# Gates o and z of the eighth head as seven products of blocks: the dense part, the attention's sums, and new orders

## The chip, the cores and the metric

The kernel runs on one core of a Trainium2 chip. A core has engines that each run their own list of instructions in order: TensorE (PE) multiplies matrices into PSUM, VectorE (DVE) and ScalarE (ACT) work on elements, GpSimd (POOL) does small things and issues those transfers that add into their target, and SyncE (SP) issues most other transfers (DMA). They wait for each other by semaphores. The metric is the device time of one execution in microseconds (us). The kernel before takes 1486.5 us, the median of three runs (1485.95 to 1486.61).

## The reference

Two layers work on 512 latent tokens of width 1024, with 256 context tokens beside them. Layer 0 mixes a long convolution (hyena) and a grouped attention; layer 1, which the change touches, is an mLSTM with 8 heads, run over the tokens in both directions. Cut to the second layer:

```python
q, k, v, o, z, gates = split(h @ w_in)          # o, z: 8 heads x 256 columns each
C = a_prev * C + (vc * a).T @ kc                # state of a head, chunk by chunk
num = s @ vc + w_prev * (C @ qc)
den = sum(s) + w_prev * (nvec @ qc)
h = num / max(abs(den), exp(-m))
h = (h_forward + h_backward) * sigmoid(o)
h = rms_norm(h, head_norm)
y = (h * silu(z)) @ w_out
x = x + gate * rms_norm(y, g_post)
```

So each head needs two gates from the layer's input: o (512 tokens x 256 columns) and z (the same), products with K = 1024. They are used only at the head's end.

## The kernel before, in words

Every fp32 product is made of three products of split numbers: a value is cast to a rounded part (names with h: `wh`, `hTh`, `vh`; a cast on ACT) and the rest (names with l: `wl`, `hTl`, `vl`; a subtraction on DVE), and `mm3` (L1013) multiplies h x h, h x l and l x h into PSUM. So each weight tile that arrives (`wr` or `ch`, 128 x 1024, 512 KB) costs one cast on ACT and one subtraction on DVE.

The program has regions: start, hyena, attention, the first output projection, the dense part of layer 1 (`l1a`), the heads (`l1b`) and the second output projection (`out1`). Each operation of a region is recorded, and `play()` (L993) issues them in an order that a table of numbers, `ORDERS`, writes out per region. All instructions therefore carry one line of the source, L998, and are told apart by their tiles. A second table says which buffer each tile gets.

In the dense part, `gates_oz(h)` (L2482) makes o and z of heads 0 to 6 together as a 2 x 2 problem of blocks. The tokens are halved, K is halved, and instead of eight block products it makes seven: the token operands are sums of blocks (`F3`, `F5`, `F6`, `D1`, made once), the weight operands are blocks or sums of blocks. The sums of weights (`o_sums` in DRAM, four per head) are made early in the program by `oz_sums` (L1633), eight steps, each one transfer per head: a copy on SP's queue or an accumulating transfer on POOL's. One of the seven products (`product`, L2469) is 2 token blocks x 4 k-blocks x 3 = 24 matmuls of 256 columns. The results are combined by sums on DVE, go through tanh or silu on ACT, and are put away in DRAM (`oz_scratch`).

`heads(h, H, N, before)` (L2544) runs head h. Per direction it forms the decay matrix `E`, the scaled keys `ka`, five state products v, ka (`pj`), the state `C` on DVE, its split `Ch` (ACT) and `Cl` (DVE), and for each of four token blocks a product v, E and a product C, q (`pm`), joined in `num`. Then `normed` rescales by the denominator into `hh`, multiplies with the gate `so`, takes squares (`hj`), the root (`hst`, `hrs`), and multiplies with `zs`; `result` transposes hh and puts it away in `y_scratch`. Between these, `fill()` takes pieces of work from a list: the next head's projections, or, in head 7, which has no next head and whose gates are not made in the dense part, its own gates. Those are plain products: `load_w` of two weights, four token blocks for each gate, 24 matmuls of 256 columns for each. Head 7 also makes the rows of the output modulation (`row`: 16 small matmuls each from 1 MB tiles of `w_mod`; `spread` sends a row to all tokens).

`out1` multiplies the heads' results with `o_w_out`, again with seven block products. Its operands come from `y_scratch` (`yraa`, `yrab`, `yfh`, `yfl`, the new content of `hTh`, `hTl`) and need many DVE subtractions of 128 x 512; the heads' region ends with its first two products (`p1`, `q7`).

Of the kernel before, what the change touches and what calls it, by code (L numbers as in the profile page):

```python
# [7 lines left out]
F32 = mybir.dt.float32  # L8
# [6 lines left out]
P = 128  # L15
# [136 lines left out]
class Ctx:  # L152
# [570 lines left out]

SLOTS = {
    "xt@0": [
        3, 5, 4, 0, 2, 1, 5, 3, 4, 0, 1, 5,
    ],
# [2166 lines left out]
```

## Time and profile before

| what | us |
|---|---|
| median of 3 runs | 1486.5 (1485.95 to 1486.61) |
| profiled execution | 1486.4 |
| its span | 1484.6 |
| 865 to 910: start of the dense part | PE busy 40.87 of 45, DVE 40.30 |
| 1320 to 1344: end of head 6 | PE 22.46 of 24, DVE 17.67, DMA share 0.89 |
| 1476 to 1484.6: after the last matmul | PE 0.31, DVE 5.17 |

The page names groups by engine, output tile and input tiles; `pj`, `pm`, `qst` and the like are names of the program. A row of a group ends with the idle time of the engine just before these instructions and with what ended most of it. A row of a timeline begins with the start and the duration of an instruction, and ends, in brackets, with the idle time before it. Matmuls overlap: their records are longer than the distance between their starts, so the starts tell the rate.

### The profile page before, as it was taken

The numbers are of one execution on the slowest core, as the hardware profiler recorded it, in microseconds if no ns is written. First come the engines' busy times: TensorE is split into PE (matmuls) and PEld (weight loads), VectorE is DVE, ScalarE is ACT, GpSimd is POOL, SyncE is SP. The second block draws the span as 40 slices with busy tenths as digits, with TensorE's granted clock in tenths as the row PEclk, the third lists the DMA queues.
The fourth block names the chain that finished last, engine by engine and source line by source line (L and its number), as shares of the span: only waits on it lengthen the run. The fifth ranks groups of instructions, "written<-read, shape, count | busy, mean of one in ns | idle before, by whom it ended". The sixth has DMA issues, their size and how long they took to land. (4 is left out here: it accounts for less than half of the span.)

```text
span 1484.6 us, 25597 instructions
## 1 busy us (share of the span) xinstructions
PE 1448.9 (98%) x10122; PEld 1320.5 (89%) x10122; DVE 1071.1 (72%) x1971; ACT 778.8 (52%) x1587; POOL 95.2 (6%) x141
## 2 busy tenths in 40 slices
PE   7999999999999999999999989999999999999997
PEld 5888998989998998989997779999999999989776
DVE  6687777887865666668334899666777777778698
ACT  5643443344435444446332567655766666766554
POOL 1100000001000000000000100000000101110000
PEclk9999999999999999999999999999999999999999
DMA  9655556557331121233463343676654647476575
GB/s 380 212 139 151 142 138 165 147 127 185 86 103 43 55 96 47 90 118 104 152 217 98 114 144 129 228 257 211 221 166 114 161 126 166 141 199 179 203 256 215
DMA packets 63687, 230.93 MB, mean 156 GB/s; under 512 B 7707, under 2 KB 9243, under 8 KB 60784
## 3 DMA queue, kind: packets, MB, share of 16 engines
q1 hardware_dynamic: 55000, 198.63, 38.9%
q0 software_dynamic: 7696, 29.50, 11.3%
q8 instruction: 79, 1.29, 0.3%
q10 hardware_dynamic: 872, 1.18, 0.2%
q14 instruction: 40, 0.33, 0.1%
HBM read 207.23 MB, written 68.19 MB: 186 GB/s over the span
## 5 line engine op out<-in xcount | busy, mean ns | idle before, releaser
L998 PE MATMUL pj<-wl,hTh 128*128 128x256 f32 (+2 forms) x1104 | 315.4, 291 | 1.9 <-DVE wl L998 1.9
L998 PE MATMUL pj<-wh,hTh 128*128 128x256 f32 (+2 forms) x1104 | 316.2, 293 | 0.8 <-ACT qjunk L998 0.4
L998 PE MATMUL pj<-wh,hTl 128*128 128x256 f32 (+2 forms) x1104 | 313.8, 291 | 0.0
L998 PE MATMUL pj<-hTh,wh 128*128 128x512 f32 (+1 forms) x832 | 286.7, 347 | 0.1
L998 PE MATMUL pj<-hTl,wh 128*128 128x512 f32 (+1 forms) x832 | 285.5, 344 | 0.6 <-DVE hTl L998 0.6
L998 PE MATMUL pj<-hTh,wl 128*128 128x512 f32 (+1 forms) x832 | 285.2, 345 | 0.0
L998 DVE TENSOR_TENSOR wl<-wr,wh 128x1024 fp32r<-128x1024 f32 (+1 forms) x154 | 187.6, 1222 | 48.5 <-ACT wh L998 45.7
L998 PEld LDWEIGHTS pj<-wl,hTh 128*128 128x128 f32 x1104 | 206.9, 189 | 7.4 <-DVE wl L998 2.9
L998 PEld LDWEIGHTS pj<-wh,hTh 128*128 128x128 f32 x1104 | 205.9, 188 | 7.4 <-issue 2.0
L998 PEld LDWEIGHTS pj<-wh,hTl 128*128 128x128 f32 x1104 | 206.0, 188 | 4.3 <-issue 1.1
L998 ACT CAST wh<-wr 128x1024 fp32r<-128x1024 f32 (+1 forms) x154 | 159.0, 1044 | 95.5 <-PE pj L998 61.7
L998 PEld LDWEIGHTS pj<-hTh,wh 128*128 128x128 f32 x832 | 156.6, 189 | 19.2 <-DVE vl L998 0.9
L998 PEld LDWEIGHTS pj<-hTh,wl 128*128 128x128 f32 x832 | 156.3, 188 | 18.2 <-DVE wl L998 0.2
L998 PEld LDWEIGHTS pj<-hTl,wh 128*128 128x128 f32 x832 | 156.7, 189 | 17.4 <-DVE hTl L998 0.9
L998 DVE TENSOR_TENSOR PTl<-pj,PTh 128x384 fp32r<-128x384 f32 (+1 forms) x80 | 41.1, 525 | 18.8 <-ACT PTh L998 18.3
L998 ACT CAST PTh<-pj 128x384 fp32r<-128x384 f32 (+1 forms) x80 | 35.5, 458 | 30.6 <-PE pj L998 30.0
L998 DVE TENSOR_TENSOR wl<-ch,wh 128x1024 fp32r<-128x1024 f32 x28 | 34.2, 1221 | 24.1 <-ACT wh L998 24.0
L998 DVE TENSOR_REDUCE mx<-s 128x1 f32<-128x768 f32 (+1 forms) x48 | 37.2, 774 | 11.4 <-PE s L998 11.2
L998 PE MATMUL pm<-Rh,dfa 128*128 128x256 f32 (+1 forms) x192 | 44.9, 305 | 0.0
L998 POOL DMA_DIRECT2D o_sums<-in_o_w_in x28 | 22.8, 814 | 333.9 <-DMA o_sums<-in_o_w_in 167.2
L998 DVE TENSOR_TENSOR med<-big 128x512 f32<-128x512 f32 (+1 forms) x48 | 40.4, 865 | 5.0 <-ACT big L998 4.7
L998 PE MATMUL s<-dfa,qTh 128*128 128x256 f32 (+1 forms) x160 | 42.8, 338 | 0.7 <-ACT hdh L998 0.6
(397 smaller groups left out, 3250.3 us busy)
## 6 DMA issues: line engine op xcount, KB each, us to landing
wr<-in_e_w_in SPq DMA_DIRECT2D x52, 512.0 KB, 5.0
wr<-in_o_w_in SPq DMA_DIRECT2D x50, 512.0 KB, 6.4
o_sums<-in_o_w_in POOLq DMA_DIRECT2D x28, 512.0 KB, 6.7
ch<-o_sums SPq DMA_DIRECT2D x21, 512.0 KB, 4.8
wh<-in_w_mod SPq DMA_DIRECT2D x10, 1024.0 KB, 8.4
wl<-in_w_mod SPq DMA_DIRECT2D x9, 1024.0 KB, 7.6
wr<-in_e_w_out SPq DMA_DIRECT2D x16, 512.0 KB, 4.0
w_sums<-in_o_w_out POOLq DMA_DIRECT2D x16, 512.0 KB, 7.6
```

The lines of the kernel that those rows point to most:

```text
L998: x = fn(*a, **k)
```

## The change

The eighth head's gates are made as the other seven heads' gates are: `gates_oz` runs for 8 heads in the dense part, and head 7 loads them from `oz_scratch` at its start as the others do. Its four sums of weights are made later than the others', in the attention: with each second of its first sixteen steps one of the eight steps of `oz_sums` is issued, for head 7 alone. Head 7's list of work for `fill()` keeps only the modulation rows. As z now comes through ACT's silu and not through (tanh + 1) times z, the constant in the norm is the same for all heads.

The tables are new for the attention (3147 entries, before 3139), the dense part (1904, before 1701) and the heads (3657, before 3871); `out1` has the same 426 in another order. In all, PE has 168 matmuls of 256 columns more in the dense part and 192 fewer in the heads.

```diff
@@ -1624,14 +1625,14 @@
-    osum = nc.dram_tensor("o_sums", [7, 4, P, 4, 256], F32).ap()
+    osum = nc.dram_tensor("o_sums", [8, 4, P, 4, 256], F32).ap()
...
-    def oz_sums(step):
-        for h in range(7):
+    def oz_sums(step, heads=range(7)):
+        for h in heads:
...
@@ -2042,6 +2043,8 @@
         todo = list(plan[n])
+        if n % 2 and n < 16:
+            oz_sums(n // 2, (7,))
         for b in range(2):
...
@@ -2257,7 +2260,7 @@
-    ozd = nc.dram_tensor("oz_scratch", [7, 2, P, 4, 256], F32).ap()
+    ozd = nc.dram_tensor("oz_scratch", [8, 2, P, 4, 256], F32).ap()
...
@@ -2512,7 +2515,7 @@
-    for h in range(7):
+    for h in range(8):
         gates_oz(h)
...
@@ -2546,29 +2549,15 @@
         so = T(mr, "so", (P, 4, 256))
         zs = T(mr, "zs", (P, 4, 256))
         work = []
+        SP.dma_start(so, ozd[h, 0])
+        SP.dma_start(zs, ozd[h, 1])
         if N:
             N.load()
             N.load_v()
-            SP.dma_start(so, ozd[h, 0])
-            SP.dma_start(zs, ozd[h, 1])
             work = [(N.key, 0), (N.key, 1), (N.query,)] + [(N.value, i) for i in (4, 5, 0)] + [(N.turned,)] + [(N.value, i) for i in (1, 2, 3)]
         else:
-            wo = load_w(ow[4 * h + 2])
-            wz = load_w(ow[4 * h + 3])
-
-            def out_gate(i):
-                ps = PJ()[:, :256]
-                proj_tok(wo, i, ps)
-                S.activation(so[:, i], ps, AF.Tanh, scale=0.5)
-
-            def gate_z(i):
-                ps = PJ()[:, :256]
-                proj_tok(wz, i, ps)
-                S.activation(zs[:, i], ps, AF.Tanh, scale=0.5)
-                V.scalar_tensor_tensor(zs[:, i], zs[:, i], 1.0, ps, ALU.add, ALU.mult)
-
             row, spread = gate_rows(gg1, gg1[:, 0], 1, 1)
-            work = [(out_gate, i) for i in range(4)] + [(row, 0)] + [(gate_z, i) for i in range(4)] + [(spread, 0), (row, 1), (spread, 1)]
+            work = [(row, 0), (row, 1), (spread, 0), (spread, 1)]
...
@@ -2667,7 +2656,7 @@
-            rstd(rs, ss, 4 * 256, tmp, div=4.0 if N else 16.0)
+            rstd(rs, ss, 4 * 256, tmp, div=4.0)
...
@@ -473,365 +474,365 @@
-        72, 73, 74, 9, 155, 158, 2, 12, 13, 14, 156, 6, 10, 88, 0, 18, 19, 20, 21, 22, 23, 24, 25, 26, 27, 28, 29, 30, 31, 32, 33, 34, 35, 36, 11,
...
+        155, 73, 2, 6, 12, 3, 72, 7, 9, 10, 13, 74, 11, 8, 18, 19, 15, 20, 21, 45, 46, 47, 48, 49, 50, 51, 52, 53, 54, 55, 56, 57, 58, 59, 60, 61, 62,
...
```

Three places of the order. The first is PE in the last head, at the products of the state and q of its first direction (`pm` from `Ch`, `Cl`, `qh`, `ql`). `pj` from `wh`, `wl` with `hTh`, `hTl` are gate products; `pj` from `vh` and `kal` is a state product; `pm` from `vh`, `vl` and `Eh`, `El` is a product of v and the decay matrix. Before:

```order
L998 MATMUL pm_11992<-Ch_11983,qh_11836 128x258
L998 MATMUL pm_11992<-Cl_11984,qh_11836 128x258
L998 MATMUL pj_11987<-wl_2360_11949,hTh 128x256
L998 MATMUL pj_11987<-wh_2359_11948,hTl 128x256
L998 MATMUL pj_12000<-wh_2359_11948,hTl 128x256
L998 MATMUL pj_12000<-wh_2359_11948,hTh 128x256
L998 MATMUL pj_11994<-vh_11834,kal_11971 128x258
L998 MATMUL pm_11992<-Ch_11983,ql_11837 128x258
L998 MATMUL pj_12000<-wl_2360_11949,hTh 128x256
L998 MATMUL pj_12000<-wh_2359_11948,hTl 128x256
L998 MATMUL pj_12000<-wh_2359_11948,hTh 128x256
```

And now:

```order
L999 MATMUL pm_12224<-Ch_12215,qh_12070 128x258
L999 MATMUL pm_12224<-Cl_12216,qh_12070 128x258
L999 MATMUL pm_12224<-Ch_12215,ql_12071 128x258
L999 MATMUL pm_12230<-Ch_12221,qh_12070 128x258
L999 MATMUL pm_12230<-Cl_12222,qh_12070 128x258
L999 MATMUL pm_12230<-Ch_12221,ql_12071 128x258
L999 MATMUL pm_12236<-Ch_12227,qh_12070 128x258
L999 MATMUL pm_12236<-Cl_12228,qh_12070 128x258
L999 MATMUL pm_12229<-vh_12068,Eh_12193 128x258
L999 MATMUL pm_12229<-vl_12069,Eh_12193 128x258
L999 MATMUL pm_12229<-vh_12068,El_12194 128x258
```

The gate matmuls that stood between the C, q products are gone, and three token blocks' products of C and q stand one behind another.

The second is DVE at the end of the last head, where `hh` is rescaled with `hrs`; PE's transposes wait for it. Before:

```order
L998 SCALAR_TENSOR_TENSOR hh_12055<-num_2430_12019,dn_12047,hh_12055 128x256
L998 SCALAR_TENSOR_TENSOR hh_12055<-so_11946,hh_12055 128x256
L998 TENSOR_SCALAR hst_12065<-hss_12060 128x4
L998 SCALAR_TENSOR_TENSOR hh_12055<-hh_12055,hrs_12066,zs_11947 128x256
L998 SCALAR_TENSOR_TENSOR zs_11947<-zs_11947,pj_12048 128x256
L998 SCALAR_TENSOR_TENSOR hh_12055<-hh_12055,hrs_12066,zs_11947 128x256 x2
L998 SCALAR_TENSOR_TENSOR zs_11947<-zs_11947,pj_12041 128x256
L998 SCALAR_TENSOR_TENSOR hh_12055<-hh_12055,hrs_12066,zs_11947 128x256
L998 TENSOR_TENSOR gg_1586_11172<-pm_12049,gg_1586_11172 128x512
```

And now:

```order
L999 SCALAR_TENSOR_TENSOR hh_12273<-num_2446_12246,dn_12272,hh_12273 128x256 x2
L999 SCALAR_TENSOR_TENSOR hh_12273<-so_12180,hh_12273 128x256 x3
L999 TENSOR_TENSOR wl_2493_12293<-wr_12294,wh_2492_12292 128x1024
L999 TENSOR_SCALAR hst_12283<-hss_12278 128x4
L999 TENSOR_TENSOR wl_2493_12293<-wr_12295,wh_2492_12292 128x1024
L999 SCALAR_TENSOR_TENSOR hh_12273<-hh_12273,hrs_12284,zs_12181 128x256 x4
L999 TENSOR_TENSOR hTl<-cvo_12277,hTh 128x256
```

The gate's own two multiplications (`zs` from `pj`) are gone, and two subtractions for weight splits (`wl`) of the output projection stand ahead of the rescaling.

The third is POOL in the attention, where `rq` is a small step of the queries' norm. Before:

```order
L998 TENSOR_TENSOR rq_4330<-qst_4329,mhalf 128x12
L998 TENSOR_TENSOR rq_4368<-qst_4367,mhalf 128x12
L998 TENSOR_TENSOR rq_4472<-qst_4471,mhalf 128x12
L998 TENSOR_TENSOR rq_4599<-qst_4598,mhalf 128x12
L998 DMA cs_4773<-y_scratch 128x2x768
```

And now:

```order
L999 TENSOR_TENSOR rq_4330<-qst_4329,mhalf 128x12
L999 TENSOR_TENSOR rq_4368<-qst_4367,mhalf 128x12
L999 DMA o_sums<-in_o_w_in 128x1024 x4
L999 TENSOR_TENSOR rq_4472<-qst_4471,mhalf 128x12
L999 TENSOR_TENSOR rq_4599<-qst_4598,mhalf 128x12
L999 DMA cs_4773<-y_scratch 128x2x768
```

Four accumulating transfers (128 x 1024) stand between the second and the third `rq`. On SP's queue four copies are added around them, the second and third of which wait for an accumulation.

More of the change, by code (lines that the diff above doesn't have):

```diff
@@ L725 @@
     "xt@0": [
-        3, 5, 4, 0, 2, 1, 5, 3, 4, 0, 1, 5,
+        1, 4, 3, 5, 0, 2, 4, 1, 3, 5, 2, 4,
     ],
     "wr@1": [
[4 rows of a table removed]
[4 rows of a table added]
     ],
@@ L737 @@
     "sst@0": [
+        0, 1, 4, 2, 3, 5,
+    ],
+    "rs@0": [
         0, 1, 2, 3, 4, 5,
     ],
-    "rs@0": [
-        0, 1, 4, 3, 2, 5,
-    ],
     "pj@2": [
-        0, 1, 0, 1, 2, 3, 0, 2, 1, 3, 2, 0, 1, 3, 2, 0, 1, 3, 3, 0, 1, 2, 0, 3, 1, 1, 3, 1, 0, 2, 3, 1, 0, 2, 0, 1, 3, 2, 0, 1, 2, 3, 1, 3, 2, 0, 1,
-        3, 2, 0, 3, 1, 2, 0, 3, 1, 0, 2, 3, 1, 0, 2, 2, 1, 0, 3, 2, 1, 0, 0, 3, 2,
+        0, 2, 0, 2, 3, 1, 0, 3, 2, 1, 3, 0, 2, 1, 3, 0, 2, 1, 1, 0, 2, 3, 0, 1, 2, 2, 1, 2, 0, 3, 1, 2, 0, 3, 0, 2, 1, 3, 0, 2, 3, 1, 2, 1, 3, 0, 2,
+        1, 3, 0, 1, 2, 3, 0, 1, 2, 0, 3, 1, 2, 0, 3, 3, 2, 0, 1, 3, 2, 0, 0, 1, 3,
     ],
@@ L750 @@
     "pm@3": [
[4 rows of a table removed]
[4 rows of a table added]
     ],
     "g@4": [
-        1, 0, 1, 0, 1, 0, 1, 0,
+        0, 1, 0, 1, 0, 1, 0, 1,
     ],
     "x0s@4": [
-        1, 0, 1, 0, 1, 0, 1, 0,
+        0, 1, 0, 1, 0, 1, 0, 1,
     ],
@@ L765 @@
     "med@4": [
[3 rows of a table removed]
[3 rows of a table added]
     ],
     "big@4": [
-        1, 0, 1, 1, 0, 1, 1, 0, 1, 1, 0, 1, 1, 0, 1, 1, 0, 1, 1, 0, 1, 1, 0, 1,
+        0, 1, 0, 0, 1, 0, 0, 1, 0, 0, 1, 0, 0, 1, 0, 0, 1, 0, 0, 1, 0, 0, 1, 0,
     ],
     "rt@6": [
-        1, 0, 0, 1, 0, 1, 0, 0, 1, 1, 0, 1, 1, 0, 1, 0, 1, 1, 0, 1, 0, 1,
+        0, 1, 1, 0, 1, 0, 1, 1, 0, 0, 1, 0, 0, 1, 0, 1, 0, 0, 1, 0, 1, 0,
     ],
     "gs@6": [
-        0, 0, 2, 1, 0, 2, 1, 0, 2,
+        0, 0, 1, 2, 0, 1, 2, 0, 1,
     ],
     "qTl@6": [
-        0, 2, 0, 1, 2, 0, 1, 2, 0,
+        0, 1, 0, 2, 1, 0, 2, 1, 0,
     ],
     "qTh@6": [
-        0, 0, 2, 1, 0, 2, 1, 0, 2,
+        0, 0, 1, 2, 0, 1, 2, 0, 1,
     ],
@@ L798 @@
     "rq@6": [
-        1, 2, 3, 0, 1,
+        2, 3, 0, 1, 2,
     ],
     "s2@8": [
-        1, 0, 1, 0, 0, 1, 1, 0, 0, 1, 0, 1, 1, 1, 0, 1, 0, 1, 1, 0, 1, 0, 1, 1, 0, 1, 0, 1, 1, 0, 0, 1, 0, 0, 1, 1, 0, 0, 1, 0, 1, 0, 0, 1, 1, 0, 1,
-        0,
+        0, 1, 0, 1, 1, 0, 0, 1, 1, 0, 1, 0, 0, 0, 1, 0, 1, 0, 0, 1, 0, 1, 0, 0, 1, 0, 1, 0, 0, 1, 1, 0, 1, 1, 0, 0, 1, 1, 0, 1, 0, 1, 1, 0, 0, 1, 0,
+        1,
     ],
     "mx@6": [
-        1, 2, 0, 3, 2, 1, 3, 0, 2, 1, 0, 3, 2, 1, 0, 2, 3, 1, 0, 2, 3, 1, 0, 2, 3, 1, 0, 2, 1, 3, 0, 2, 3, 0, 1, 3, 2, 1, 0, 2, 3, 1, 2, 0, 3, 1, 0,
-        2,
+        0, 1, 3, 2, 1, 0, 2, 3, 1, 0, 3, 2, 1, 0, 3, 1, 2, 0, 3, 1, 2, 0, 3, 1, 2, 0, 3, 1, 0, 2, 3, 1, 2, 3, 0, 2, 1, 0, 3, 1, 2, 0, 1, 3, 2, 0, 3,
+        1,
     ],
     "sm@6": [
-        0, 3, 1, 2, 3, 0, 2, 1, 3, 0, 1, 2, 0, 3, 1, 2, 0, 3, 1, 2, 0, 3, 1, 2, 0, 3, 1, 2, 3, 0, 1, 2, 0, 1, 3, 0, 2, 1, 3, 2, 0, 1, 2, 3, 1, 0, 2,
-        3,
+        2, 1, 0, 3, 1, 2, 3, 0, 1, 2, 0, 3, 2, 1, 0, 3, 2, 1, 0, 3, 2, 1, 0, 3, 2, 1, 0, 3, 1, 2, 0, 3, 2, 0, 1, 2, 3, 0, 1, 3, 2, 0, 3, 1, 0, 2, 3,
+        1,
     ],
@@ L816 @@
     "xt@9": [
-        1, 0, 1, 0, 1, 0, 1,
+        0, 1, 0, 1, 0, 1, 0,
     ],
     "pj@10": [
[5 rows of a table removed]
[5 rows of a table added]
     ],
     "pm@11": [
[5 rows of a table removed]
[5 rows of a table added]
     ],
     "yraw@9": [
-        1, 1, 0, 0, 0, 1, 1, 1,
+        0, 0, 1, 1, 1, 0, 0, 0,
     ],
@@ L848 @@
     "xn@9": [
-        1, 0, 1, 2, 2, 0, 1, 2, 0, 1, 0, 2,
+        0, 1, 0, 2, 2, 1, 0, 2, 1, 0, 1, 2,
     ],
```

26 lines of the change are left out of this document (13 added, 13 removed), and 751 rows, old and new, of tables (ORDERS, SLOTS).

## The prediction

> **What bounds the kernel now.** I read the page first, then a table of stretches, then starts of single instructions, then waits.
>
> ```profile
> PE 1448.9 (98%) x10122; PEld 1320.5 (89%) x10122; DVE 1071.1 (72%) x1971; ACT 778.8 (52%) x1587; POOL 95.2 (6%) x141
> ```
>
> TensorE (PE) is busy nearly all the time, so a change must take work from it or keep it from waiting. The busy time hides waits, though: a matmul's record is longer than the distance to the next one. By stretches (columns: PE, PEld, DVE, ACT, POOL, each busy us and count, then clock, DMA share, GB/s):
>
> ```profile
> 910.00:1050.00 140.00, 140.00 (x1154) 138.83 (x1152) 94.91 (x117) 83.47 (x119) 0.00 (x0) 1.00 0.64 216
> 1050.00:1320.00 270.00, 269.03 (x1951) 252.96 (x1950) 205.00 (x418) 183.00 (x452) 30.64 (x53) 1.00 0.56 155
> 1344.00:1394.00 50.00, 49.55 (x398) 46.29 (x397) 38.18 (x88) 31.00 (x80) 3.20 (x3) 1.00 0.58 182
> 1394.00:1426.00 32.00, 29.54 (x142) 20.11 (x140) 26.05 (x35) 18.76 (x27) 0.00 (x0) 1.00 0.80 277
> 1426.00:1476.00 50.00, 49.64 (x212) 39.59 (x212) 43.94 (x60) 24.91 (x38) 1.87 (x2) 1.00 0.67 233
> ```
>
> The first is the dense part with the seven-product gates, the second heads 0 to 5 and most of 6, the third the last head, the fourth the start of the output projection, the fifth its rest. In all five PE is the fullest engine, and in the dense part VectorE (DVE) has 45 us free of 140. Only from 1394 to 1426 does PE wait visibly, with DVE at 26 of 32.
>
> What a matmul costs is read from starts:
>
> ```profile
> 1343.85 0.28 PE L998 MATMUL pm<-Ch,ql 128*128 128x258 f32 x1
> 1343.97 0.28 PE L998 MATMUL pj<-wh,hTl 128*128 128x256 f32 x1
> ...
> 1349.00 0.29 PE L998 MATMUL pj<-wl,hTh 128*128 128x256 f32 x1
> 1349.12 0.28 PE L998 MATMUL pj<-wh,hTl 128*128 128x256 f32 x1
> 1349.24 0.28 PE L998 MATMUL pj<-wh,hTh 128*128 128x256 f32 x1
> ...
> 1475.45 0.39 PE L998 MATMUL pj<-wh,ybh 128*128 128x512 f32 x1
> 1475.68 0.40 PE L998 MATMUL pj<-wl,ybh 128*128 128x512 f32 x1
> 1475.92 0.39 PE L998 MATMUL pj<-wh,ybl 128*128 128x512 f32 x1
> ```
>
> So 0.12 us for 256 or 258 columns (0.119 over longer runs) and 0.234 for 512. The first row is also a mark: the last product of state C and q of head 6. From there (1343.97) to the last matmul's end of issue (1475.92 + 0.23) pass 132.2 us.
>
> DVE the same way:
>
> ```profile
> 1319.70 1.22 DVE L998 TENSOR_TENSOR wl<-wr,wh 128x1024 fp32r<-128x1024 f32 x1
> 1320.84 0.48 DVE L998 SCALAR_TENSOR_TENSOR C<-C,apb,pj 128x258 f32<-128x258 f32 x1
> 1321.23 0.42 DVE L998 TENSOR_TENSOR Cl<-C,Ch 128x258 fp32r<-128x258 f32 x1
> 1321.57 0.69 DVE L998 SCALAR_TENSOR_TENSOR E<-pm,E 128x512 f32<-128x512 f32 x1
> ```
>
> Each next one starts 0.08 us before the recorded end of the one ahead, so an instruction takes its duration less 0.08 (1.14, 0.39, 0.34).
>
> **The change part by part.** *Matmuls.* The last head's two gates took 2 weights x 4 token blocks x 8 k-blocks x 3 = 192 matmuls of 256 columns, between the mark and the head's end. They become 7 products x 8 x 3 = 168 in the dense part: 168 x 0.119 = +20.0 there, 192 x 0.119 = -22.8 in the head, net **-2.8 us**. In the dense part the new head's gates also bring DVE 7 weight splits (7 x 1.14) and 7 sums of 128x512 (about 0.61 each): 12.3 us beside 20.0 of PE. The row of 910 to 1050 is made of just such heads and has DVE at 68%: hidden. Its seven loads of 512 KB come at the rate of the seven heads before it, at a DMA share of 0.64: hidden too; uncovered, each would cost up to a split's 1.14.
>
> *The last head without its gates.* This is the step that decides. From the mark to the last matmul PE has, before, 242 matmuls of 256 columns, 78 of 258, 338 of 512, 32 of the modulation row and 20 transposes: 28.8 + 9.4 + 79.1 + 1.9 + 1.3 = 120.5. In the changed kernel only the 242 differ; they are 51: 97.7. Before, then, PE waited 132.2 - 120.5 = **11.7 us**. DVE's work between the same points hardly shrinks. These groups of DVE in the last head (busy, mean ns, then the idle time before them and its releaser) price it:
>
> ```profile
> L998 DVE SCALAR_TENSOR_TENSOR num<-pm,cq,num 128x258 f32<-128x258 f32 x11 | 5.2, 481 | 0.5 <-PE pm L998 0.3
> L998 DVE TENSOR_TENSOR wl<-wr,wh 128x1024 fp32r<-128x1024 f32 x4 | 4.9, 1218 | 0.0
> L998 DVE SCALAR_TENSOR_TENSOR hh<-hh,hrs,zs 128x256 f32<-128x256 f32 x8 | 3.7, 481 | 1.3 <-POOL hrs L998 1.2
> L998 DVE TENSOR_TENSOR Cl<-C,Ch 128x258 fp32r<-128x258 f32 x8 | 3.4, 424 | 4.4 <-ACT Ch L998 4.4
> ...
> L998 DVE SCALAR_TENSOR_TENSOR E<-pm,E 128x512 f32<-128x512 f32 x2 | 1.4, 687 | 1.2 <-ACT E L998 1.2
> ...
> L998 DVE TENSOR_TENSOR hTl<-vh,hTh 128x768 fp32r<-128x768 f32 x1 | 1.0, 953 | 0.0
> ...
> L998 DVE TENSOR_SCALAR hst<-hss 128x4 f32<-128x4 f32 x2 | 0.3, 171 | 2.2 <-ACT hj L998 2.2
> ```
>
> Up to the last rescaling of hh, the changed DVE has 79 instructions: 24 on hh and 9 num and 8 C at 0.40, 8 Cl at 0.34, 4 weight splits at 1.14, 4 of 768 columns at 0.87, 4 of E at 0.60, and 18 smaller ones (3.7): 33.1 us. PE in front of the transposes that need hh: 51 x 0.119 + 78 x 0.12 + 39 x 0.234 + 2.6 = 27.2. Before, the same count gave DVE 36.1 (87 instructions) against PE's 45.5. So the head turns from bound by PE, with 9 us to spare on DVE, to bound by DVE by 6. It does not recover at once: on to the last part of the first operand of the output projection (yfl), DVE has 117 instructions, 61.1 us, and PE 53.7 in front of its use. PE must wait **at least 7.4 us** between the mark and there even if DVE never waits. (Before: DVE 66.7, PE 77: no bound.)
>
> To that come DVE's own waits, which PE's surplus of work used to cover. The rows show 4.4 (Cl for ACT's Ch), 2.2 (hst), 1.2 (hrs) and 1.2 (E); the waits (total, times, longest) count the first and add one on a weight cast:
>
> ```profile
> DVE Cl L998 <- ACT Ch L998: 4.4, 3, 2.3
> DVE wl L998 <- ACT wh L998: 3.0, 1, 3.0
> ```
>
> Together 12.0. None of these instructions is removed. The bounds: nothing of it, if the new order puts other work between each pair, and all of it. I take three quarters, 9.0, because in the new order PE's rows of the head stand nearly without gate matmuls between them, while DVE's rows do have hTl and weight splits between. PE then waits 7.4 + 9.0 = 16.4 after the mark instead of 11.7: **+4.7 us**.
>
> *The order ahead of the mark.* One stall stands in head 6, on a copy of ACT behind the gate weights' loads and splits:
>
> ```profile
> 1328.61 0.39 PE L998 MATMUL pm<-Ch,qh 128*128 128x258 f32 x1 [1.54 <-ACT num L998]
> ```
>
> The loads and splits of the gate weights, four of each, are gone from here. Between 0 and 1.5 may be won; I take half, **-0.8**.
>
> *The sums in the attention.* Eight DMAs more. The rows of POOL, of SP and of the weight that comes behind:
>
> ```profile
> 465.15 2.27 POOL L998 TENSOR_TENSOR rq<-qst,mhalf 128x12 f32<-128x12 f32 x1 [18.88 <-DVE qst L998]
> 530.62 2.27 POOL L998 TENSOR_TENSOR rq<-qst,mhalf 128x12 f32<-128x12 f32 x1 [63.19 <-DVE qst L998]
> ```
>
> ```profile
> L998 POOL DMA_DIRECT2D o_sums<-in_o_w_in x28 | 22.8, 814 | 333.9 <-DMA o_sums<-in_o_w_in 167.2
> ```
>
> ```profile
> o_sums<-in_o_w_in POOLq DMA_DIRECT2D x28, 512.0 KB, 6.7
> ```
>
> ```profile
> 478.65 0.33 SPq L998 DMA_DIRECT2D wr<-in_e_w_in  x1
> ...
> 509.32 0.33 SPq L998 DMA_DIRECT2D y_scratch<-dec  x1
> ```
>
> ```profile
> 530.60 1.04 ACT L998 CAST wh<-wr 128x1024 fp32r<-128x1024 f32 x1
> ```
>
> POOL's four accumulating issues stand between the second and the third rq, where POOL idles 63 us. Each waits for a copy of SP's queue, a copy for the accumulation ahead: pairs of 6.7 us each, a copy taken at as long as an accumulation. From 467.4 on, the first three pairs take until about 496. The fourth copy stands behind the transfer of 509.32 on SP's queue, so that POOL issues its last near 517, 13 us before rq at 530.6. The load of 478.65 stands behind three of the copies, of which the third can go near 489; its data are cast at 530.6. Cost nothing; without that cover, PE would stand for what rq or the cast is late.
>
> The sum: -2.8 + 4.7 - 0.8 = +1.1 on the profiled run's own 1486.4, hence **1487.5 us**; the median of the runs is 1486.5, so nothing is to be corrected. A measurement of this kernel can tell about 0.2% (3.0 us) from no change; the forecast lies inside.
>
> One rule of the Trainium skill speaks against this change more than my sum does. The page "VectorE: DVE Perf Modes", section "The DRAIN you can't avoid", says that after each DVE instruction the pipe drains and the next does not start until it is empty, and advises fewer instructions. By it, a DVE instruction would cost its whole duration. The trace disagrees: 1320.84 is before 1319.70 + 1.22. By the rows the floor of PE's wait is 7.4, by the rule it would be 16.8, the third rival below.
>
> **The rivals.**
>
> *Faster: the waits stay as they were.* The new order was made for this head; if it fills DVE's gaps, PE waits the 7.4 and some 3 on the modulation row and transposes, under the 11.7 of before: -2.8 - 1.3 - 1.5 (the whole stall) = 1480.8; with waits as before, 1482. For it: heads 0 to 5 keep PE at 269.0 of 270 with DVE at 76%. Against: the last head asks for 33.1 us of DVE beside 27.2 of PE, which none of those do. It decides below 12.3 us of waits. Chance 0.22.
>
> *Slower: the bare head.* The head is a chain of round trips, a product into PSUM, C on DVE, Ch on ACT, Cl on DVE, the next product; with no gate matmuls between, PE stands at each. The three waits on Ch took 4.4, so 1.5 each; if the whole 12.0 shows, PE waits 19.4: -2.8 + 7.7 = 1491.3; if all eight Cl wait so, 7.3 more, 1498.6. For it: the changed order of PE has the C, q products of the first direction in a row with nothing else between. Against: ACT is at 31 of 50 there and can answer at once. It decides from 18.3 us of waits on. Chance 0.26, at 1492.5.
>
> *DVE without overlap.* If 0.08 us more went with each of the 117 instructions, DVE's sum would be 70.5, the floor 16.8 instead of 7.4: 1496.9. Of the rule above the rows bear out nothing for independent instructions. Chance 0.02.
>
> *The attention held up.* If the pairs of DMAs take twice as long beside the weights' loads, the fourth ends near 565 and rq waits 35 us: 1520. The idle slices there make it unlikely: chance 0.02.
>
> *The gates don't move at all* is excluded by the order of PE, which has 51 instead of 242.
>
> **How the numbers follow.** My forecast, within 0.2%, has 0.48; the faster rival 0.22, the slower ones 0.26 + 0.02 + 0.02. So faster 0.22, same 0.48, slower 0.30. The forecast's own range, from half to the whole of DVE's waits, is 1484.5 to 1490.5. To hold 8 in 10, it reaches to 1482, where waits stay as before, and to 1493, past the price of the bare head.
>
> **What would show it.** After the change, the stretch from the mark (near 1363) to the last matmul should last 97.7 + 16 = 114 us, with DVE over 85% busy from the mark to hh and PE's waits named DVE hh, Cl or wl; the last head's PE busy share should fall while the end stays. If PE waits there under 12 us in all, my three quarters were too many; over 18, the bare head is right. Waits on rq near 530 or at 865 to 906 beyond those of before would show a cost I set to nothing. The dense part must be 20 us longer, with PE full; more than that, and DVE or DMA bounds it.

## The result, and the profile after

The changed kernel takes **1494.34 us** (median of 4 runs, 1493.62 to 1497.16), beside 1486.55 (1485.95 to 1486.69) for the kernel before on the same chip: a ratio of 1.0057, 95% interval 1.0045 to 1.0070. It is 0.57% slower. Forecast was 1487.5 in a range of 1482 to 1493, so the range missed it by a little over 1 us and the likeliest case by 7.

The profiled execution took 1494.06 us (span 1492.3, before 1484.6). The page's first row hardly differs from the one before; PE is still the full engine:

```profile
PE 1452.2 (97%) x10098; PEld 1322.4 (89%) x10098; DVE 1076.4 (72%) x1977; ACT 783.8 (53%) x1587; POOL 99.2 (7%) x145
```

So the ledger was made by stretches with ends that both kernels have: the wait that opens the dense part (845), the first product of the dense gates (906), the mark (the last C, q product of head 6) and the last matmul. Columns as in the forecast's table of stretches: PE, PEld, DVE, ACT, POOL, then PE's granted clock, DMA share, GB/s. The kernel before:

```profile
845.90:906.50 60.60, 53.73 (x341) 47.70 (x339) 54.73 (x106) 39.61 (x70) 4.87 (x10) 1.00 0.36 123
906.50:1343.90 437.40, 434.89 (x3301) 416.64 (x3302) 320.98 (x573) 285.94 (x612) 33.09 (x58) 1.00 0.60 180
1343.90:1476.10 132.20, 128.93 (x750) 106.10 (x749) 108.36 (x181) 74.77 (x143) 5.08 (x5) 1.00 0.67 224
```

The kernel after:

```profile
845.40:905.90 60.50, 53.18 (x324) 47.13 (x322) 54.57 (x104) 39.31 (x70) 4.89 (x10) 0.97 0.37 123
905.90:1367.60 461.70, 458.11 (x3486) 440.11 (x3487) 332.81 (x592) 297.02 (x627) 33.41 (x59) 1.00 0.61 184
1367.60:1483.40 115.80, 109.83 (x558) 85.16 (x556) 102.63 (x173) 69.31 (x130) 5.29 (x4) 0.99 0.67 226
```

| stretch | before, us | after, us | difference |
|---|---|---|---|
| up to the opening wait (845) | 845.9 | 845.4 | -0.5 |
| start of the dense part | 60.6 | 60.5 | -0.1 |
| dense gates and heads to the mark | 437.4 | 461.7 | +24.3 |
| mark to last matmul | 132.2 | 115.8 | -16.4 |
| behind the last matmul, to the span's end | 8.5 | 8.9 | +0.4 |

The moved matmuls alone would be +20.0 and -22.8. The stretch ahead of the mark has 4.3 us too much, the one behind it 6.4 too much. Two things stand out in the profile after. The first is one long wait of PE in head 3, of which the kernel before has no counterpart:

```profile
1221.23 0.27 PE L999 MATMUL pm<-c_ident,cvo 128*128 128x128 f32 x1
1224.27 0.58 PE L999 MATMUL pm<-Ch,qh 128*128 128x258 f32 x1 [2.77 <-ACT Ch L999]
1224.65 0.41 PE L999 MATMUL pj<-wh,hTh 128*128 128x256 f32 x1
1224.87 0.41 PE L999 MATMUL pj<-wl,hTh 128*128 128x256 f32 x1
1225.08 0.41 PE L999 MATMUL pj<-wh,hTl 128*128 128x256 f32 x1
```

The second stands in the same rows: behind the wait, matmuls of 256 columns start 0.21 us apart, not 0.12. By stretches of about 3 us, the granted clock (the third column from the end) is 0.50 there, and at two more places:

```profile
879.80:882.90 3.10, 3.10 (x15) 3.10 (x14) 3.03 (x5) 1.38 (x2) 0.00 (x0) 0.50 0.02 5
1224.40:1227.70 3.30, 3.30 (x14) 3.07 (x15) 2.26 (x7) 1.40 (x4) 0.00 (x0) 0.50 0.44 179
1381.40:1384.70 3.30, 3.30 (x17) 3.30 (x17) 2.64 (x6) 2.29 (x7) 0.00 (x0) 0.50 1.00 412
```

PE is "busy" all through these 3 us and does half the work, so each costs about 1.5 us, which no busy share shows. Each lies right behind waits of PE: 2.14 us at 876, 2.77 at 1221, and 0.46 and 1.05 at 1378 to 1381. In the profile of the kernel before, no matmul ran at half clock behind the first 21 us, though it has single waits of 1.6 and 1.5. The mean clocks of the whole executions agree: 0.993 to 0.995 after, 0.996 to 0.999 before.

**Why PE waited at 1221.** PE wants Ch, which ACT casts. ACT works in order and stood in front of a weight that had not arrived:

```profile
1222.87 1.04 ACT L999 CAST wh<-wr 128x1024 fp32r<-128x1024 f32 x1 [3.98 <-DMA wr<-in_o_w_in]
1223.82 0.40 ACT L999 CAST Ch<-C 128x258 fp32r<-128x258 f32 x1
```

That load belongs to head 4 and has nothing to do with the moved gates. The changed order of SP's queue puts it behind a second load of `decay` (the row of 1203.58 holds both), and that one waits 6.0 us for ACT to be done with `E`:

```profile
1203.58 6.77 SPq L999 DMA_DIRECT2D decay<-nc_scratch  x2
1210.44 0.38 SPq L999 DMA_DIRECT2D zs<-oz_scratch  x1
1210.93 0.59 SPq L999 DMA_DIRECT2D wr<-in_o_w_in  x1
```

Issued at 1210.93, it lands at 1222.8: 11.9 us for 512 KB, in a stretch where the share of the DMA engines is 0.98 to 1.03. Being behind one waiting transfer cost ACT 4.0 us, PE 2.8, and then 1.5 for the clock.

**Behind the mark**, PE's waits are many and small, and the names differ from those forecast. The largest at the end of head 6:

```profile
1378.63 1.05 PE L999 MATMUL pm<-c_ident,hh 128*128 128x128 f32 x5 [0.46 <-DVE hh L999]
...
1381.07 0.43 PE L999 MATMUL pm<-vh,Eh 128*128 128x258 f32 x1 [1.05 <-ACT y L999]
```

(ACT reads the transposes of hh out of `pm` into `y`, and PE's next product waits for that.) ACT makes y late because five casts for the output projection stand ahead of it, and the first of these waited for rows of `y_scratch`:

```profile
1375.50 0.83 ACT L999 CAST hTh<-vh 128x768 fp32r<-128x768 f32 x1 [1.88 <-DMA vh<-y_scratch]
...
1378.87 1.05 ACT L999 CAST wh<-wr 128x1024 fp32r<-128x1024 f32 x1
1379.81 0.62 ACT L999 CAST Eh<-E 128x512 fp32r<-128x512 f32 x1
1380.33 0.69 ACT L999 ACTIVATE y<-pm,hnc 128x512 f32<-128x512 f32 x1
```

Those rows of `y_scratch` were issued from 1365.3 on, beside two accumulating transfers of `w_sums` (sums of the output projection's weights) that POOL had issued just ahead, at 1361.19.

### The profile page after: what moved, and what is told of

It reads as the page before. It is cut to its first block, busy times and chain, and to the rows that moved or that the text cites. A ratio compares the mean times of both kernels' runs of the same rounds, so it can differ in the third digit from the quotient of the medians.

```text
span 1492.3 us, 25616 instructions
## 1 busy us (share of the span) xinstructions
PE 1452.2 (97%) x10098; PEld 1322.4 (89%) x10098; DVE 1076.4 (72%) x1977; ACT 783.8 (53%) x1587; POOL 99.2 (7%) x145
## 3 DMA queue, kind: packets, MB, share of 16 engines
q8 instruction: 79, 1.29, 0.3%
## 5 line engine op out<-in xcount | busy, mean ns | idle before, releaser
L999 PE MATMUL pj<-wh,hTh 128*128 128x256 f32 (+2 forms) x1056 | 304.5, 294 | 3.4 <-DVE wa L999 2.1
L999 PE MATMUL pj<-wl,hTh 128*128 128x256 f32 (+2 forms) x1056 | 303.0, 291 | 0.6 <-DVE wl L999 0.6
L999 PE MATMUL pj<-wh,hTl 128*128 128x256 f32 (+2 forms) x1056 | 302.2, 293 | 0.6 <-DVE hTl L999 0.6
L999 PEld LDWEIGHTS pj<-wh,hTh 128*128 128x128 f32 x1056 | 198.4, 190 | 9.6 <-ACT wh L999 3.2
L999 PEld LDWEIGHTS pj<-wl,hTh 128*128 128x128 f32 x1056 | 199.4, 190 | 4.8 <-DVE wl L999 1.2
L999 PEld LDWEIGHTS pj<-wh,hTl 128*128 128x128 f32 x1056 | 198.3, 190 | 4.8 <-DVE hTl L999 1.0
L999 DVE TENSOR_TENSOR wl<-ch,wh 128x1024 fp32r<-128x1024 f32 x32 | 39.1, 1221 | 30.5 <-ACT wh L999 30.5
L999 ACT CAST wh<-ch 128x1024 fp32r<-128x1024 f32 x32 | 33.5, 1047 | 36.2 <-PE pm L999 17.1
L999 POOL DMA_DIRECT2D o_sums<-in_o_w_in x32 | 26.1, 817 | 379.3 <-DMA o_sums<-in_o_w_in 193.9
```

Of the source, the lines that this page charges most:

```text
L999: x = fn(*a, **k)
```

## The experiments

All runs were timed against the kernel before on the same chip. In the diffs, `_move(region, i, b)` takes recorded operation i of a region's order and issues it just ahead of operation b.

| kernel | median, us (range) | before beside it | ratio (95%) |
|---|---|---|---|
| after | 1494.34 (1493.62 to 1497.16) | 1486.55 | 1.0057 (1.0045 to 1.0070) |
| kept_busy | 1494.29 (1493.26 to 1494.53) | 1486.75 | 1.0052 (1.0036 to 1.0069) |
| wr_early | 1488.96 (1488.28 to 1490.12) | 1486.75 | 1.0015 (1.0006 to 1.0025) |
| wa_first | 1494.50 (1491.45 to 1497.18) | 1486.75 | 1.0053 (1.0032 to 1.0074) |
| light | 1495.03 (1493.42 to 1496.37) | 1486.75 | 1.0056 (1.0041 to 1.0071) |
| sums_early | 1486.17 (1484.72 to 1488.68) | 1485.16 | 1.0013 (1.0003 to 1.0022) |
| casts_late | 1490.78 (1488.82 to 1493.28) | 1485.16 | 1.0038 (1.0025 to 1.0051) |
| both_ends | 1489.84 (1489.18 to 1490.73) | 1485.16 | 1.0031 (1.0019 to 1.0042) |
| all_moves | 1488.85 (1486.91 to 1490.58) | 1485.16 | 1.0020 (1.0009 to 1.0032) |
| wr_again | 1488.92 (1486.90 to 1489.71) | 1486.06 | 1.0019 (1.0010 to 1.0028) |
| sums_wa | 1485.55 (1483.95 to 1487.64) | 1486.06 | 0.9998 (0.9989 to 1.0007) |
| best_wa | 1485.44 (1484.05 to 1487.04) | 1486.06 | 0.9991 (0.9982 to 1.0000) |

The kernel before itself differs by 1.6 us from chip to chip, so kernels timed on different chips are compared by ratio.

### wr_early: the weight load of head 4 ahead of the waiting transfer

```diff
+_move("l1b", 1837, 1848)   # SP: load of wr (head 4) ahead of the second load of decay
```

> The changed kernel with one weight load of head 4 (behind which ScalarE's cast and the cast of the state Ch of head 3 stand at 1222.9) moved ahead of the second load of decay on SP's queue. If the load was late because it was issued at 1210.9, behind a load that waits for ScalarE: it goes at about 1207.3 and lands by 1217, the wait of 2.8 us at 1221 goes, and with it the half clock there: 4.4 us less, 1489.9; if the half clock costs nothing, 2.8 less, 1491.5. If the transfers around it (DMA share 0.98 to 1.03 from 1210 to 1225) decide, it lands hardly earlier and the time stays within 1 us of 1494.3.

One transfer moved ahead of one other gives back 1.0057 - 1.0015 = 0.42%, about 6 us of the 8. In its profile the load goes out at 1205.98, and ACT comes to its cast without a wait:

```profile
1217.54 1.03 ACT L1007 CAST wh<-wr 128x1024 fp32r<-128x1024 f32 x1
1218.48 0.40 ACT L1007 CAST Ch<-C 128x258 fp32r<-128x258 f32 x1
```

PE has no wait there and no half clock. The load also takes less time, 8.1 us from issue to landing and not 11.9. The repeat on another chip (wr_again, below) gives 1.0019; the two agree within 0.6 us, and the intervals leave about 2 us either way. The theory expected 4.4 us; the profile's stretch from the first gate product to the mark shortens from 461.7 us to 457.7 (457.5 in wr_again), by 4.0 to 4.2. The median gains more than that. The mean clock over the runs fits: it rises from 0.9945 to 0.9965, which is 3 us of 1490, beside the wait of 2.8.

### kept_busy: the clock without the order

Dummy products fill three waits of PE (before the Ch of 1221, before 876, where PE waits for `wa`, a small addition on DVE, and around the transposes of hh at the end of head 6). They write to a PSUM tile that the next true product overwrites; no order changes.

```diff
+FILL = {("l1b", 1603): (1603, 1650, 14), ("l1a", 18): (92, 18, 18),
+        ("l1b", 3322): (3332, 3332, 3), ("l1b", 3345): (3332, 3332, 6)}
...
+            if (name, i) in FILL:
+                o, m, n = FILL[name, i]
+                ...
+                for _ in range(n):
+                    tc.keep_in_program_order(fm(out, am[1], am[2][:, :c], start=True, stop=True))
```

> The changed kernel with matmuls thrown in while TensorE waits: 18 small ones in the wait of 2.1 us at 876, 14 of 256 columns in the wait of 2.8 us at 1221, 3 and 6 of 258 columns in those of 0.5 and 1.1 us at 1378 and 1380. They write PSUM that is overwritten; the waits stay. If the three stretches at half clock (880, 1224, 1381, about 3.2 us each) come from these waits and cost 1.6 us each: mean clock 0.999 instead of 0.995, and 4.8 us less, about 1489.5. If the half clock falls into time that is lost to other engines anyway: the clock is restored and the time stays within 1 us of 1494.3. If waits don't set the clock: 0.995 as before.

The median did not move, though the mean clock rose to 0.9968 and two of the three stretches at half clock are gone from the profile. So the cost of the three cannot simply be added up. The profile says where the gain went. Where a wait was well filled (876), the clock held:

```profile
877.90:880.90 3.00, 3.00 (x23) 3.00 (x24) 2.93 (x4) 0.41 (x1) 0.00 (x0) 1.00 0.02 5
880.90:883.90 3.00, 3.00 (x25) 2.96 (x23) 3.00 (x4) 3.00 (x5) 0.00 (x0) 1.00 0.00 0
```

and the heads up to the third run 2.5 us ahead of the kernel after, of which 1.0 was there before the dummies (at 859). At 1221 the dummies left 1.4 us of wait, and the half clock came all the same (1223.3 to 1226.8). And what was won ahead is lost at the end of head 6: the first transposes of hh stand at 1377.99, in the kernel after at 1377.84.

```profile
1377.99 0.33 PE L1013 MATMUL pm<-c_ident,hh 128*128 128x128 f32 x1 [1.88 <-DVE hh L1013]
```

ACT waited 3.6 us for `y_scratch` there. So the end of head 6 is a second place that sets the time, not by PE's work but by when the loads land. sums_early and casts_late, further down, take that up.

### wa_first: the wait at 876 alone

```diff
+_move("l1a", 8, 13)
+_move("l1a", 11, 13)
```

> The changed kernel with two small additions of VectorE at the start of the dense part (wa, which free the PSUM that TensorE waits for at 876) moved ahead of one of 256 and one of 1024 columns. If the order of VectorE makes that wait: 2.1 us become 1.1, the half clock at 880 goes, 2.6 us less, about 1491.7. If VectorE's sum from 863 to 884 is the limit there, the wait moves on: the half clock may go, at most 1.6 less, 1492.7 to 1494.3.

The wait fell and the profile has no half clock at 880, but the median stays, and the four runs spread from 1491.45 to 1497.18. In the profiled one, three stretches further on ran at half clock (1224.4 to 1227.8; 1381.4 to 1388.3, twice the usual length; 1432.6 to 1436.0). It could not be told apart from the kernel after.

### light: DVE relieved in the last head

Leaves out six subtractions that make `hTl` for the output projection, 4.1 us of DVE, so part of the output is computed from old numbers.

```diff
+            if name == 'l1b' and i in (3485, 3488, 3494, 3596, 3592, 3590):
+                continue
```

> The changed kernel without six subtractions of VectorE at the end of the last head (the low parts hTl of the output projection's first operands; its result is therefore not the reference's): 4.1 us less of VectorE between the last products of head 6 and the first operand yfl. If VectorE's sum bounds the last head (floor 7.4 us of TensorE's waits): the floor falls to 3.3 and the time by 3 to 4 us, to about 1490.8. If round trips of TensorE, VectorE and ScalarE bound it: less than 1 us, above 1493.3.

Nothing came of it: from the mark to the first transposes of head 7's hh 39.65 us (after 39.45), to the last matmul 115.4 (after 115.6), and the median is not lower. So the sum of DVE's work is not what PE waits for in the last head, at least while the other waits stand as they do here. The wait that stands out here is the one on ACT:

```profile
1383.92 0.58 PE L1001 MATMUL pm<-vh,Eh 128*128 128x258 f32 x1 [1.96 <-ACT y L1001]
```

### sums_early and casts_late: two reasons for the late y

The loads of `y_scratch` come late, or ACT's five casts are in the way. Both kernels contain wr_early's move.

```diff
+_move("l1b", 3233, 3240)   # POOL: the last two accumulations of w_sums ahead of
+_move("l1b", 3231, 3240)   # its last select over decay, which waits for a load
```

> Two orders differ from the kernel after: the weight load of head 4 stands ahead of the second decay load on SP's queue (as in wr_early, which took 1488.96 us), and the last two accumulating transfers of w_sums (512 KB each, issued by POOL at 1355.6 in wr_early's profile, beside the loads of y_scratch issued at 1359.8 to 1366) are issued ahead of POOL's last select over decay, which waits 17.5 us: at about 1337, where the DMA engines have a share of 0.13. Theory (the six loads of y_scratch come late because the sums share the engines with them; ACT waits 1.49 us and DVE 1.29 for them at 1369.5, and everything behind in their queues, up to y, is late): the loads land about 2 us earlier, both waits go, PE's wait of 1.29 for y shrinks to at most 0.5: 1487.0 to 1488.2. Rival (what makes y late is not the loads but the casts of ACT that stand ahead of y): the loads land earlier, and PE's wait for y stays within 0.4 us: 1488.6 to 1489.4.

```diff
+for i, b in ((3272, 3224), (3484, 3348), (3487, 3319), (3493, 3416), (3530, 3374), (3589, 3429)):
+    _move("l1b", i, b)     # ACT: Eh earlier, five casts behind y
+for i, b in ((3273, 3225), (3486, 3339), (3489, 3339), (3485, 3365), (3488, 3397), (3494, 3397)):
+    _move("l1b", i, b)     # DVE: El earlier, five subtractions behind it
+_move("l1b", 3553, 3554)   # PE: first product of these rows, 12 us later
```

> As wr_early (1488.96 us), and in the orders of ACT and DVE around the end of head 6 the work on the rows of y_scratch for the block products (on ACT five casts, 3.9 us together, of them 3.1 behind the wait for the loads and ahead of Eh and y; on DVE five subtractions, 4.2 us) stands behind Eh, El and both casts of y, spread over the 20 us that follow; PE's first product of them stands 12 us later. Theory (ACT's queue makes y late): PE's waits for hh (0.43) and y (1.29) go, and with them the 1.5 us at half clock that followed at 1375.9: 1486.0 to 1487.6, first transposes of head 7's hh 2 to 3 us earlier than in wr_early. Rival (bare recurrence of head 7, or DVE, full 9.5 of 10 us from 1380 to 1390, takes the gain back): y comes 2 us earlier, but the waits for Ch, Cl, num and hTl behind it grow by as much: 1488.4 to 1490.

With the sums at 1334.7 instead of 1355.6, the loads of `y_scratch` land 3.1 to 4.1 us after their issue, where they took 7.7 to 8.5 in wr_early. ACT and DVE no longer wait for them, and PE's wait for y falls from 1.29 to 0.21. Of sums_early's timeline, the transfers on POOL:

```profile
1334.68 1.67 POOL L1009 DMA_DIRECT2D w_sums<-in_o_w_out  x2
```

the first cast of those rows on ACT, with no idle time ahead of it:

```profile
1365.99 0.82 ACT L1009 CAST hTh<-vh 128x768 fp32r<-128x768 f32 x1
```

and PE's product that waits for y:

```profile
1371.39 0.39 PE L1009 MATMUL pm<-vh,Eh 128*128 128x258 f32 x1 [0.21 <-ACT y L1009]
```

From the mark to the first transposes of head 7 it takes 36.7 us, in wr_early 39.3. From the mark to the start of the last matmul the gain is 1.9 us (113.8 against 115.7), the size that the theory expected. But wr_early's profile has a stretch at half clock in this piece (1375.9 to 1379.3). The profile of wr_again, the same kernel, has none there and takes 114.6, which leaves 0.9 us for the loads alone. The ratio does not stand clear of wr_early's, since the runs spread over 4 us, with mean clocks from 0.996 to 0.998; times the first chip's 1486.75 it gives 1488.7, the time that the rival named. So the theory's mechanism is there, and its size in time is not shown by this run.

The other edit did harm: casts_late lies above both of its ranges, and both_ends (next) is 3.7 us above sums_early on the same chip, from which it differs by the moves of casts_late alone. With the casts moved back, y is there in time (0.22), and the waits turn up behind it, on the copies of ACT and DVE that the casts now delay. Waits of PE in casts_late's timeline:

```profile
1373.24 0.39 PE L1020 MATMUL pm<-vh,Eh 128*128 128x258 f32 x1 [0.22 <-ACT y L1020]
...
1378.80 0.38 PE L1020 MATMUL pm<-Ch,qh 128*128 128x258 f32 x1 [1.25 <-ACT Ch L1020]
1379.60 0.58 PE L1020 MATMUL pm<-Cl,qh 128*128 128x258 f32 x1 [0.42 <-DVE Cl L1020]
1388.06 0.39 PE L1020 MATMUL pm<-Ch,qh 128*128 128x258 f32 x1 [0.76 <-ACT num L1020]
1392.30 0.39 PE L1020 MATMUL pm<-Cl,qh 128*128 128x258 f32 x1 [0.95 <-DVE Cl L1020]
```

The half clock came too, 3.4 us later than in wr_early (1379.3 to 1382.7), and the first transposes of head 7 stand 40.5 us behind the mark, not 2 to 3 us earlier than wr_early's 39.3. So ACT's order does make y late, but changing it is no cure: the casts then hold up the copies behind y. Of the two moves, that of the load helped and that of the work did not.

### both_ends and all_moves

both_ends is wr_early with both edits, all_moves adds the moves of wa_first.

> wr_early with both edits, the sums early and the casts late. Theory (each has its own share: the loads land earlier, so that the casts, wherever they stand, never hold up ACT or DVE): no more than 0.6 us better than casts_late alone, since the casts no longer stand in front of y: 1485.6 to 1487.4. Rival (the two are worth their sums): 1.0 to 2.0 us better than casts_late.

> both_ends and, ahead of head 0, the two moves of wa_first (the weights wa split first, which took away the wait of 2.14 us at 876 and left 1.5 us at head 3 in its profile). Theory (that wait is PE's alone, and its half clock with it, and nothing behind it takes the gain back once the ends of the heads are mended): 1.0 to 2.5 us below both_ends, 1483.5 to 1486, so faster than the kernel before (1486.75). Rival (what is gained ahead is lost at the end of head 6 to transfers and casts that don't come earlier, as in kept_busy and wa_first): within 0.7 us of both_ends.

With the casts moved, the early sums bring 0.9 us, between the theory (no more than 0.6) and its rival (1.0 at least); the moves of wa bring 1.0 more, the low end of what was expected. Neither step is clear of the noise. Neither kernel comes near the kernel before, and the casts are why: sums_wa, the next kernel, is all_moves without them and has 0.9998 (at most 1.0007), all_moves 1.0020 (at least 1.0009). In all_moves' profile it takes 41.8 us from the mark to head 7's transposes, with 6.8 us at half clock from 1377 on.

### wr_again, sums_wa, best_wa: the parts together, on one chip

sums_wa is wr_early, sums_early and wa_first in one; best_wa also moves a subtraction of DVE that frees a weight buffer.

```diff
+_move("l1a", 8, 13)        # sums_wa and best_wa
+_move("l1a", 11, 13)
+_move("l1b", 1837, 1848)
+_move("l1b", 3233, 3240)
+_move("l1b", 3231, 3240)
+_move("l1b", 3599, 3596)   # best_wa alone
```

> The same kernel as wr_early, on the chip that runs the next two, so that the effect of the early sums is read beside it and not across chips. Theory: 0.15% above the kernel before, as wr_early was (1.0006 to 1.0025). In its profile the waits of PE for y (1.3 us) and hh (0.4) at the end of head 6, and a stretch at half clock behind them in some executions.

> wr_early, the early sums of sums_early and the two moves of wa_first together; the casts stay where after has them. Theory (three separate waits, each with a chance of a stretch at half clock behind it: 1221, 1375 and 876): the sums are worth 2 us (mark to last product 113.8 us in sums_early's profile, 115.7 in wr_early's), the moves of wa 1.5 us, so 2 to 4 us below wr_early on the same chip, and 0 to 0.15% below the kernel before. Rival (what is gained ahead is lost at the end of head 6): within 1 us of wr_early.

> sums_wa, and on DVE the subtraction that frees a weight buffer at 1399.5 (in sums_early's profile) stands 2 us earlier, ahead of three others, so that the load issued at 1400.8 into it, which ACT waits 3.98 us for and PE 1.33 us at 1405.9, starts up to 2 us sooner. Theory: that wait goes, 0.5 to 1.3 us below sums_wa. Rival (the load is held by the crowded engines, DMA share 0.83 to 1.00 from 1400 to 1410, or the gain is lost to the waits for yfh and yfl that follow): within 0.4 us of sums_wa.

On the same chip sums_wa is 3.4 us below wr_again and level with the kernel before (0.9998). best_wa is level with sums_wa, as its rival said: counted from the mark, the load goes out 0.8 us sooner (40.0 against 40.7) and lands at the same time (45.7 against 45.8), so its buffer is not what held it. The crowded DMA engines (share 0.87 to 1.03 while it was under way) are the likely cause, which no run tested. PE's wait for it stays at 0.6 us. Its ratio, 0.9991 with an interval up to 1.0000, is the lowest of all, but too near to 1 to call it faster than the kernel before.

The stretches of sums_wa against the table above:

```profile
843.90:902.90 59.00, 51.94 (x323) 45.48 (x322) 54.39 (x104) 39.04 (x70) 4.56 (x10) 1.00 0.36 127
902.90:1360.30 457.40, 456.48 (x3486) 438.81 (x3487) 333.67 (x592) 297.09 (x627) 34.09 (x59) 1.00 0.62 187
1360.30:1473.70 113.40, 108.26 (x558) 83.79 (x556) 102.50 (x173) 69.16 (x130) 5.91 (x5) 1.00 0.64 226
```

No half clock in any. The middle is 437.4 + 20.0, to the tenth. The last stretch is 132.2 - 18.8, so of the 22.8 us of matmuls that left it, 4.0 came back as waits.

What the half clock costs is best seen in a piece that is the same, order for order, in wr_again and sums_early, from the opening wait of the dense part to its first gate product. Of wr_again:

```profile
845.60:906.10 60.50, 53.16 (x324) 47.15 (x322) 54.57 (x104) 39.26 (x70) 4.88 (x10) 0.97 0.37 123
```

Of sums_early:

```profile
843.70:902.70 59.00, 51.64 (x323) 45.55 (x323) 54.40 (x104) 39.32 (x70) 4.60 (x10) 1.00 0.37 127
```

Both have the wait of 2.14 us at 876. Behind it wr_again ran 3 us at half clock and sums_early did not: 60.5 against 59.0. So the wait makes the half clock possible and not certain.

What decides can be read from the traces' own records of the granted clock. In all thirteen profiles, any two changes of the clock lie a whole number of steps of 3.413 us apart, and each stretch at half clock between two matmuls lasts 3.413 us or, in wa_first and all_moves, once twice that. So the clock is set anew every 3.413 us, and the grid of these windows lies differently over the program in each execution. PE's busy time in single windows (a window has 3.41 us):

| profile | window, us | PE busy, us | clock in the next window |
|---|---|---|---|
| after | 876.10 to 879.51 | 1.27 | 0.50 |
| wr_again | 877.08 to 880.49 | 1.45 | 0.50 |
| light | 878.54 to 881.95 | 1.43 | 0.50 |
| sums_early | 875.54 to 878.95 | 1.75 | 1.00 |
| casts_late | 877.57 to 880.98 | 1.71 | 1.00 |
| wr_early | 863.91 to 867.32 | 1.57 | 0.50 |
| both_ends | 863.89 to 867.30 | 1.58 | 0.50 |
| after | 865.86 to 869.27 | 1.93 | 1.00 |

The first five are the same wait of 2.14 to 2.16 us. In sums_early and casts_late the window begins 0.5 us inside it, so that a part of the wait counts for the window ahead. The last three are two waits of about 0.85 and 1.0 us, which stand in all thirteen profiles; in wr_early and both_ends one window holds both whole, and only there did the half clock follow. Over all windows at full clock from 60 us on (5393), half clock always followed where PE stood idle for 1.84 us or more of the window (21 windows, 13 of them at the program's end) and never where it stood idle for less than 1.39; in between it followed 9 of 22. PE's ends are modelled, so these two bounds are rough.

With the wait cut by the moves of wa (to 0.92 us in sums_wa), none of four profiles (wa_first, all_moves, sums_wa, best_wa) has it there. In sums_wa the time up to the first gate product is no shorter than in sums_early (59.0), since most of the 1.2 us won at 876 reappear as waits at 887 (0.6) and 902 (0.3 more): the moves take away a risk, not a wait. The mean clock of the runs says the same: 0.9967 in wr_again, 0.9979 in sums_wa, 0.9984 in the kernel before beside them. 0.0012 of 1486 us is 1.8 us, about half of the 3.4 between the first two; the last stretch, 114.8 against 113.4 up to the end of the last matmul's issue, is most of the rest.

## Why the prediction was wrong, step by step

- **Gates moved, -2.8.** Right: 168 x 0.119 in the dense part. In sums_wa the middle stretch is 20.0 us longer (the stall of 1.5 in head 6 is gone there, and as much came in small waits). The dense part's own work on DVE and its loads are hidden, as said: from 905.9 to 1067.4 PE is busy for 161.4 of 161.5 us.
- **The order ahead of the mark, -0.8. This is the step that failed.** I priced the one stall of head 6 that I saw in the profile of before (1.54 at 1328.61), and it did go. I did not look for what the new order of SP's queue puts in front of what. In head 3 it puts a weight load behind a transfer that waits 6.0 us; with the half clock behind it, that cost 4.3 us of profile, and some 6 us of the median. The forecast followed the queues of POOL and SP only in the attention; the order of SP's queue could have been read in the same way for the heads.
- **The clock.** In no term. Three stretches at about 1.5 us are 4.5 us of the 7.7 in the profile. That the time would fall by as much without them, to about 1489.6 and inside the range, is not shown: kept_busy had two of the three fewer and took as long. The Trainium skill has the rule on its page "TensorE: Matmul & The Clock Gate" (section "HAM oscillation — how this bites in real kernels"): no idle gap of PE above about 3.4 us. By that rule waits of 2.1 and 2.8 us would be safe. Here they were not always safe, and two of about 0.85 and 1.0 us were enough in two profiles of thirteen (wr_early and both_ends, half clock from 867.3 to 870.7), where they fell into one window.
- **Behind the mark, +4.7.** 16.4 us of waits were forecast, 115.8 - 97.7 = 18.1 came, of which some 1.6 are half clock. (The modulation rows have 64 products in either trace, not the 32 of the forecast's sum; that makes both 11.7 and 18.1 some 1.7 us too high and leaves their difference as it is.) The size was right and the working was not. DVE's floor of 7.4 us is not what bound: with 4.1 us of DVE's work left out, nothing moved (light). Of DVE's own waits, Cl on Ch had 4.4 us before and 0.2 after. In their place came late rows of `y_scratch`, ACT's queue behind them, and the half clock; once the loads land in time, 0.9 us go, or 1.9 beside a profile with a stretch at half clock there (sums_early). The figure came near by accident.
- **The attention, 0.** Right, as far as it can be told: up to 845 the kernel after is 0.5 us ahead, less than what the clock at the program's start moves (last section).
- **The start of the dense part** was thought unchanged; its new order is worth 1.6 us (59.0 against 60.6), which the half clock at 880 hid in the profile after.
- **Rivals.** "Faster" needs the waits of before behind the mark; the mended order comes to 113.4 - 97.7 = 15.7, so it fell even there. "The bare head" comes near in time (1491.3 to 1498.6), but its mechanism is not there: PE's waits on Cl and Ch behind the mark are 0.4 and 0.2 us. "DVE without overlap" gave 1496.9; light speaks against it. The forecast quoted only half of what the page behind it says: the Trainium skill, "VectorE: DVE Perf Modes", goes on in the section "The DRAIN you can't avoid" that a next instruction that is not held starts earlier. The forecast's row (1320.84, ahead of 1319.70 + 1.22) agrees with that half. No rival named a transfer stuck behind another or the clock, which together are what happened.

What stays open: what decides on the clock behind a window in which PE stood idle for 1.4 to 1.8 us. The mended kernel still waits 4 us more behind the mark than the move of the matmuls alone would leave; the largest that have a name are those on hTl, wh, yfh and yfl at 1402 to 1420, 3.1 us together, and no run took them away.

## What to carry to other kernels

When an order is written anew, read each in-order queue around every load that someone needs: not how long the load takes, but what it now stands behind and what that waits for. One 512 KB load behind one waiting transfer cost more than the whole change was about. A wait that disappears from the engine in front may reappear behind; here, bringing data earlier helped and pushing the consumer's work later did not. And price PE's waits with the clock that can follow them: about 1.5 us on top, with a chance that grows once PE stands idle for 1.4 us or more within 3.4 us.

## What the runs showed of the hardware

- PE's granted clock was 0.50 for 3.413 us behind waits of 2.1 us (876), 2.8 us (1221), 0.5 + 1.1 us around small matmuls (1378), and in two profiles of thirteen 0.85 + 1.0 us (864 to 867). A 258-column matmul then starts 0.215 us behind the last, not 0.12. The half clock follows every window of 3.413 us in which PE stood idle for 1.84 us or more, and some of those in which it stood idle for 1.39 to 1.84. Where the windows lie differs from run to run of the same order, which alone sets them some 1.5 us apart.
- A load of 512 KB took 11.9 us from issue to landing in a stretch of DMA share 0.98 to 1.03. The same load, issued at 1205.98 in wr_early, took 8.1. Loads of 256 KB took 7.7 to 8.5 us beside two accumulating transfers (wr_early) and 3.1 to 4.1 without them (sums_early).
- Profiles of kernels that are the same up to there differ by 2 us at the opening wait of the dense part (843.7 in sums_early, 845.8 in best_wa), and these 2 us are there 20 us into the execution (the same products of `xt` and `cond` start at 19.17 and 21.21). They come from the clock: PE's transposes start 0.21 us apart at first and 0.11 later, from 15.4 us on in sums_early and from 20.5 on in best_wa, where the record of the full clock begins. Of the thirteen profiles, six have the full clock at 14.0 to 15.4 us and these products at 19.2 to 19.5; the other seven have it at 19.4 to 21.8 and the products at 20.6 to 22.5. That is as much as most of the edits here are worth, so edits were judged by stretches between two points of the program.
